# State-space tables one batch per piece of the first layer, held behind VectorE's last work

## The chip, the cores and the metric

The kernel runs on one core of a Trainium2 chip. The metric is the device time of one execution in microseconds; the time stated is the median of three runs. TensorE does the matmuls, VectorE and ScalarE the element-wise work and the reading of PSUM, GpSimd a part of the element-wise work, and SyncE issues most DMAs.

## What is computed

A network of four layers on x of [512 tokens, 2048 channels]: layer ab (gated linear attention beside forgetting attention), layer c (a state-space layer), an even layer (recurrence beside window attention) and an odd layer (two further attentions), with a norm ahead of each and one at the end. The change concerns the parameters of layer c, which depend on the weights alone:

```python
def s5_ssm(u, lam_re, lam_im, log_step, b_re, b_im, c_re, c_im, d):   # 128 groups of 16 channels, 64 states each
    step = jnp.exp(log_step)[:, None]
    mag = jnp.exp(lr * step)
    lb_re, lb_im = mag * jnp.cos(li * step), mag * jnp.sin(li * step)
    ...
    _, _, x_re, x_im = lax.associative_scan(_complex_combine, (a_re, a_im, bu_re, bu_im), axis=1)
    y = einsum('gcp,blgp->blgc', c_re, x_re) - einsum('gcp,blgp->blgc', c_im, x_im)
    return y + d * uf
```

The kernel writes the recurrence with powers of the complex factor. A table of angles holds, for the eight groups of a batch, the cosine and sine parts for 512 positions; it is the product of two small tables, so four products and two sums make it.

## The kernel before

**Projections.** Every projection is a sum of three matmuls on split operands (a high and a low part of weight and activation), `PARTS`, line 270. SyncE's queue loads a weight piece (`wraw`, three buffers), ScalarE writes its high part (`act`, line 137) and VectorE its low part (`tt`, line 140) into `whl` (four buffers), then TensorE runs 12 matmuls of 128x512 on it (`mm`, line 152), in `chunkF` (line 272) or `chunkT` (line 290). The sums stand in four PSUM banks `pj`. These loads and splits have a raised priority.

**Order.** A scheduler that simulates time sets the order of the instructions on each engine before the launch; on the chip each engine runs its own list in that order and waits by semaphores. Tiles come from a pool by name: a name has so many buffers (line 109), and a new tile takes the next buffer in the order in which the program asks for tiles, so its first writer waits for the last reader of the tile that had the buffer. `whl` has four, `hc` four, `vs` four, `fac`, `cst`, `acc`, `acc2` and `lm` one each. `after(...)` (line 159) adds a rule to the scheduler: what is issued in it comes behind the named instruction on the same engine.

**State-space parameters.** `params(o)` (line 1589) is called with o = 0 in layer ab, with 1 to 8 around the attention heads of its second half (`fox`, line 781), with 9 to 12 after the pieces of the gate, and with 13 to 20 after the eight pieces of `w_out` (line 444, the call is `beside(13 + o)`). There are 16 batches of eight groups.
- o = 0: the small tables of all batches go to memory (`s5tab`, `s5w`).
- o = 1 to 8: `s5_tables(2 * (o - 1))` (line 999) makes the tables of two batches: one load of 192 KB into `lm` (line 1004), and for each batch, on VectorE, twice `cst<-lm`, `acc<-lm` and the sum or difference `hc<-cst,acc`. The two `hc` are stored by ScalarE's queue as `s5ph` (lines 1020 and 1021).
- o = 3 to 18: `s5_batch_params(o - 3)` (line 1024) has two halves. The first loads two `vs` tiles and lets GpSimd make Z: `cst<-vs,vs` twice, `hc<-cst` twice, a store to `s5d`, and the same once more, then VectorE GG (`vs<-vs,smb`, `acc<-vs`, in the tile `acc2`), then GpSimd BB (`fac<-vs,smb`, `fac<-fac`). The profile names a tile by its tag without numbers, so GG reads as `acc` there. The second half, 32 small matmuls (`tr<-vs,fac`, `tr<-acc,fac`) and its stores, comes one call of `params` later.

`w_out` asks for a tile `acc` when it starts; GpSimd adds up squares in it (`acc<-acc,wt`) for the next norm, which reads it with eight matmuls `sc<-ones,acc` at the start of layer c. Layer c (line 1174) begins with `states(c_)` (line 1192): a chunk of 16 weight pieces by `chunkT`, whose sums ScalarE writes into two `vs` tiles (`vs<-pj,tk`), four `pj` banks at a time; the next chunk follows in the same banks. After it the recurrence of layer c reads `s5ph` and `s5d`.

## Time and profile before

| | us |
|---|---|
| median of three runs | 3410.19 (3409.04 to 3414.12) |
| the profiled execution's own time | 3407.61 |
| its span in the trace | 3405.8 |
| TensorE busy in it | 3349.1 (98%) |
| VectorE, ScalarE, GpSimd busy | 1907.8, 1337.7, 784.1 |

The profile is one execution on the chip. Times in its rows count from the start of the span. A busy TensorE is not TensorE at its peak: its granted clock is 1.00 of full speed (2.4 GHz) in most stretches and 0.96 on average between 480 and 800 us, where single runs of matmuls after a wait are at the lower level (1.2 GHz) for a part of their length. Idle time of an engine is put down to what ended it. The parameters of layer c are made from 490 us on, `w_out` of layer ab runs from about 791 to 975 us, and layer c starts with the norm at 983 us.

### The profile page before, as it was taken

To read this page: it belongs to the slowest core of one execution; us is meant where nothing else is said; L and a number is where in the kernel's file an instruction comes from. 1 tells how busy PE (TensorE), PEld (TensorE's weight loads), DVE (VectorE), ACT (ScalarE), POOL (GpSimd) and SP (SyncE) were. 2 spreads that over 40 slices of the span, in tenths; PEclk is the share of its full clock that TensorE was granted. 3 is DMA by queue.
4 is the path that set the end of the run, shared out by engine and by line. 5 is a ranking of instruction groups with operands and counts; after the bars stand their busy time and mean duration, and the time that the engine had idled before them with its cause. 6 is when DMAs were issued, how large, how long until landed. Compare 5 with 4: busy or idle time off the path is not lost.

```text
span 3405.8 us, 45778 instructions
## 1 busy us (share of the span) xinstructions
PE 3349.1 (98%) x16332; PEld 2722.4 (80%) x16332; DVE 1907.8 (56%) x3213; ACT 1337.7 (39%) x2497; POOL 784.1 (23%) x974
## 2 busy tenths in 40 slices
PE   9999999999999999999999999999999999999997
PEld 8888776777788888888888777888888788888885
DVE  5753457787556576834354655453544545647634
ACT  5443432233343333423343655232433444535532
POOL 0330364348602223200221100012110120212011
PEclk9999999999999999999999999999999999999999
DMA  5223335576634444343443223334333223332343
GB/s 156 72 69 91 87 109 159 169 218 207 206 107 132 135 144 141 116 121 118 145 127 90 66 75 90 94 120 145 105 92 81 73 65 81 80 88 75 106 120 106
DMA packets 389013, 390.01 MB, mean 115 GB/s; under 512 B 66968, under 2 KB 327448, under 8 KB 388784
## 3 DMA queue, kind: packets, MB, share of 16 engines
q1 hardware_dynamic: 362992, 354.64, 36.4%
q10 hardware_dynamic: 22464, 22.12, 1.9%
q0 software_dynamic: 3328, 10.32, 0.8%
q8 instruction: 128, 2.10, 0.3%
q14 instruction: 101, 0.83, 0.1%
HBM read 340.71 MB, written 46.25 MB: 114 GB/s over the span
## 4 chain that ended last, share of the span: by engine, by line
PE 73%; DVE 2%; POOL 1%; issue 1%; DMA 0%; DVEq 0%; ACT 0%; SPq 0%
PE pj L152 66%; PE sc L152 3%; PE po L152 3%; PE tr L156 1%; POOL wt L140 1%; DVE wk L140 0%; PE tr L152 0%; DVE hl L140 0%; DMA vs<-s5w 0%; DVE wk L1139 0%; DVE whl L140 0%; POOL cst L140 0%; DVE ha L143 0%; DVE sc L140 0%; DVE hc L143 0%
## 5 line engine op out<-in xcount | busy, mean ns | idle before, releaser
L152 PE MATMUL pj<-hl,whl 128*128 128x512 f32 x10224 | 2459.6, 398 | 14.8 <-DVE whl L140 7.3
L152 PEld LDWEIGHTS pj<-hl,whl 128*128 128x128 f32 x10224 | 1912.8, 189 | 456.3 <-DVE whl L140 10.2
L140 DVE TENSOR_TENSOR whl<-wraw,whl 128x512 fp32r<-128x512 f32 (+2 forms) x1064 | 805.3, 759 | 1082.7 <-ACT whl L137 1077.5
L137 ACT ACTIVATE whl<-wraw 128x512 fp32r<-128x512 f32 (+2 forms) x1064 | 661.5, 623 | 1353.9 <-PE pj L152 1096.6
L152 PE MATMUL pj<-whl,hl 128*128 128x512 f32 (+2 forms) x2112 | 466.1, 380 | 4.1 <-DVE whl L140 2.3
L152 PEld LDWEIGHTS pj<-whl,hl 128*128 128x128 f32 x2112 | 375.4, 191 | 81.4 <-DVE whl L140 3.1
L140 POOL TENSOR_TENSOR acc<-acc,wt 128x512 f32<-128x512 f32 x73 | 102.7, 1415 | 798.7 <-ACT wt L137 797.4
L137 ACT ACTIVATE wk<-sc,sm 128x256 f32<-128x256 f32 (+3 forms) x160 | 79.6, 502 | 90.3 <-DVE sm L148 86.8
L140 POOL TENSOR_TENSOR ha<-wk,ha 64x512 fp32r<-64x512 f32 x32 | 45.0, 1407 | 290.7 <-ACT ha L137 264.2
L140 POOL TENSOR_TENSOR wt<-wt,acc 64x508 f32<-64x508 f32 x32 | 63.9, 1995 | 181.4 <-DVE wt L140 125.7
L140 POOL TENSOR_TENSOR wt<-ha,wk 128x256 f32<-128x256 f32 x72 | 61.9, 888 | 127.4 <-PE sc L152 66.9
L152 PE MATMUL po<-pt,vs 128*128 128x128 f32 x560 | 80.0, 276 | 0.2
L152 PEld LDWEIGHTS po<-pt,vs 128*128 128x128 f32 x560 | 72.8, 192 | 3.2 <-ACT pt L137 0.8
L152 PE MATMUL sc<-ha,ha 128*128 128x128 f32 (+1 forms) x224 | 71.2, 390 | 3.5 <-DVE ha L140 2.7
L156 PE MATMUL tr<-ident,wk 128*128 128x128 f32 x416 | 71.4, 275 | 1.4 <-DVE pt L509 1.1
L137 ACT ACTIVATE pt<-tr 128x384 f32<-128x384 f32 (+3 forms) x96 | 46.7, 486 | 62.0 <-PE tr L156 60.1
L148 DVE TENSOR_SCALAR wk<-wk,sm 128x256 f32<-128x256 f32 (+3 forms) x160 | 65.4, 422 | 4.5
L140 POOL TENSOR_TENSOR fac<-wt,acc 128x512 fp32r<-128x512 f32 x8 | 10.8, 1353 | 244.3 <-ACT acc L137 130.3
L156 PEld LDWEIGHTS tr<-ident,wk 128*128 128x128 f32 x416 | 52.0, 141 | 18.8 <-issue 3.4
L137 ACT ACTIVATE ge<-ge 128x512 f32<-128x512 f32 x64 | 40.3, 630 | 66.7 <-DVE ge L140 55.7
L521 DVE TENSOR_REDUCE sm<-sc 128x1 f32<-128x128 f32 (+3 forms) x96 | 45.8, 487 | 34.1 <-PE sc L152 33.5
L140 POOL TENSOR_TENSOR cst<-vs,vs 128x256 f32<-128x256 f32 x64 | 53.5, 855 | 32.1 <-DMA vs<-s5w 18.8
(316 smaller groups left out, 2984.3 us busy)
## 6 DMA issues: line engine op xcount, KB each, us to landing
wraw<-in_l_w_in_dram SPq DMA_DIRECT2D x272, 256.0 KB, 2.8
wraw<-in_ab_w_in_dram SPq DMA_DIRECT2D x216, 256.0 KB, 2.8
wraw<-in_c_w_in_dram SPq DMA_DIRECT2D x128, 256.0 KB, 2.7
wraw<-in_l_w_out_dram SPq DMA_DIRECT2D x128, 256.0 KB, 2.9
wraw<-in_ab_w_out_dram SPq DMA_DIRECT2D x64, 256.0 KB, 3.4
wraw<-in_glu_w_dram SPq DMA_DIRECT2D x64, 256.0 KB, 2.9
wraw<-in_c_w_out_dram SPq DMA_DIRECT2D x64, 256.0 KB, 3.0
wraw<-in_l_w_in_dram SPq DMA_DIRECT2D x128, 128.0 KB, 2.3
```

Source lines behind the costliest of these rows:

```text
L137: return self.nc.scalar.activation(out, in_, func, **kw)
L140: return (eng or self.nc.vector).tensor_tensor(out, a, b, op=op)
L148: return e.tensor_scalar(out, a, s1, None, op0=op0)
L152: return self.nc.tensor.matmul(out, l, r, start=start, stop=stop)
L156: return self.nc.tensor.transpose(out, in_, self.ident[:k, :k])
L521: self.nc.vector.tensor_reduce(mx, pb[:, 0:w], axis=AX.X, op=ALU.max)
```

## The change

`s5_tables` makes one batch's table instead of two, and becomes a generator with two steps. It is called with o = 1 to 16 (so the last four tables fall among the first four pieces of `w_out`), with a load of 96 KB for each. The first step is held by `after` behind the last `tensor_tensor` that `tt` had issued on VectorE by then (`last_dve`), the second step, the two stores, behind the last instruction that `act` had issued on ScalarE (`last_act`), and it runs in the next call of `params`. In `params` the second steps that are pending now come first, then the table, then the batch.

```diff
--- before.py
+++ after.py
@@ -134,10 +134,14 @@
 
 
     def act(self, out, in_, func=AF.Copy, **kw):
-        return self.nc.scalar.activation(out, in_, func, **kw)
+        self.last_act = self.nc.scalar.activation(out, in_, func, **kw)
+        return self.last_act
 
     def tt(self, out, a, b, op, eng=None):
-        return (eng or self.nc.vector).tensor_tensor(out, a, b, op=op)
+        r = (eng or self.nc.vector).tensor_tensor(out, a, b, op=op)
+        if eng is None:
+            self.last_dve = r
+        return r
 
     def stt(self, out, a, s, b, op0, op1, **kw):
         return self.nc.vector.scalar_tensor_tensor(out, a, s, b, op0=op0, op1=op1, **kw)
@@ -996,30 +1000,31 @@
         self.own = self.cp.tile([P, 16], F32, name="own")
         nc.vector.tensor_reduce(self.own, self.ident.rearrange("p (a c) -> p c a", c=16), axis=AX.X, op=A.add)
 
-    def s5_tables(self, b0):
-
+    def s5_tables(self, b):
 
         nc, A = self.nc, ALU
-        tab = self.t("lm", [P, S])[:, 0:384].rearrange("p (b f) -> p b f", b=2)
-        self.dma.dma_start(tab, self.s5tab[b0:b0 + 2, :, 0:192].rearrange("b p f -> p b f"))
-        for b in range(2):
-            Tb = tab[:, b, 0:128].rearrange("p (i n q) -> p i n q", i=2, q=4)
-            Ta = tab[:, b, 128:192].rearrange("p (i n q) -> p i n q", i=2, q=4)
-            C, Sn = self.hd("hc"), self.hd("hc")
-            u = [self.t("cst", [P, S]), self.t("acc", [P, S])]
-            v4 = lambda ap: ap.rearrange("p (q a b) -> p q a b", q=4, a=8)
-            av = lambda i: Ta[:, i].rearrange("p n q -> p q n").unsqueeze(3).to_broadcast([P, 4, 8, 16])
-            bv = lambda i: Tb[:, i].rearrange("p n q -> p q n").unsqueeze(2).to_broadcast([P, 4, 8, 16])
+        tab = self.t("lm", [P, S])
+        self.dma.dma_start(tab[:, 0:192], self.s5tab[b][:, 0:192])
+        Tb = tab[:, 0:128].rearrange("p (i n q) -> p i n q", i=2, q=4)
+        Ta = tab[:, 128:192].rearrange("p (i n q) -> p i n q", i=2, q=4)
+        C, Sn = self.hd("hc"), self.hd("hc")
+        u = [self.t("cst", [P, S]), self.t("acc", [P, S])]
+        v4 = lambda ap: ap.rearrange("p (q a b) -> p q a b", q=4, a=8)
+        av = lambda i: Ta[:, i].rearrange("p n q -> p q n").unsqueeze(3).to_broadcast([P, 4, 8, 16])
+        bv = lambda i: Tb[:, i].rearrange("p n q -> p q n").unsqueeze(2).to_broadcast([P, 4, 8, 16])
+        with self.after([self.last_dve]):
             self.tt(v4(u[0]), av(0), bv(0), A.mult)
             self.tt(v4(u[1]), av(1), bv(1), A.mult)
             self.tt(C, u[0], u[1], A.subtract)
             self.tt(v4(u[0]), av(0), bv(1), A.mult)
             self.tt(v4(u[1]), av(1), bv(0), A.mult)
             self.tt(Sn, u[0], u[1], A.add)
-            d = self.dp.tile([P, 2, S], F32, name=self.name("s5ph"))
+        yield
+        d = self.dp.tile([P, 2, S], F32, name=self.name("s5ph"))
+        with self.after([self.last_act]):
             nc.scalar.dma_start(d[:, 0], C)
             nc.scalar.dma_start(d[:, 1], Sn)
-            self.s5ph.append(d)
+        self.s5ph.append(d)
 
     def s5_batch_params(self, b):
 
@@ -1591,15 +1596,16 @@
 
             if o == 0:
                 net.s5_params()
-            elif o <= 8:
-                net.s5_tables(2 * (o - 1))
             for b in pending:
                 with net.after([net.last]):
                     next(b, None)
             pending.clear()
+            if 1 <= o <= 16:
+                pending.append(net.s5_tables(o - 1))
+                next(pending[-1])
             if 3 <= o < 19:
                 pending.append(net.s5_batch_params(o - 3))
-                next(pending[0])
+                next(pending[-1])
         if "ab" in layers:
             h = net.layer_ab(raws, beside=params if "c" in layers else None)
             raws, acc, _ = net.w_out(h, I["ab_w_out"][0], beside=params if "c" in layers else None, **end("ab"))
@@ -1609,8 +1615,8 @@
             if "ab" not in layers:
                 net.s5_params()
                 for b in range(16):
-                    if b % 2 == 0:
-                        net.s5_tables(b)
+                    for _ in net.s5_tables(b):
+                        pass
                     for _ in net.s5_batch_params(b):
                         pass
             h = net.layer_c(raws, acc)
```

Instruction order on VectorE in the second half of layer ab, where the first tables stand (`whl<-wraw` are weight splits, `ha<-pj` evictions), before:

```order
L140 TENSOR_TENSOR cst_4050<-lm_4046 128x512
L140 TENSOR_TENSOR acc_4051<-lm_4046 128x512
L140 TENSOR_TENSOR whl_4620<-wraw_4618,whl_4620 128x512
L140 TENSOR_TENSOR ha_4572<-pj_4440,bc_230 128x512
L140 TENSOR_TENSOR hc_4048<-cst_4050,acc_4051 128x512
L140 TENSOR_TENSOR ha_4580<-pj_4441,bc_230 128x512
L140 TENSOR_TENSOR cst_4050<-lm_4046 128x512
L140 TENSOR_TENSOR acc_4051<-lm_4046 128x512
L140 TENSOR_TENSOR whl_4637<-wraw_4635,whl_4637 128x512
L140 TENSOR_TENSOR hc_4049<-cst_4050,acc_4051 128x512
L140 TENSOR_TENSOR whl_4654<-wraw_4652,whl_4654 128x512
L140 TENSOR_TENSOR cst_4063<-lm_4046 128x512
```

The same place after (the table here is the third one; four of its six instructions are shown):

```order
L141 TENSOR_TENSOR whl_4595<-wraw_4593,whl_4595 128x512
L141 TENSOR_TENSOR hc_4198<-cst_4200,acc_4201 128x512
L141 TENSOR_TENSOR whl_4612<-wraw_4610,whl_4612 128x512
L141 TENSOR_TENSOR cst_4200<-lm_4196 128x512
L141 TENSOR_TENSOR acc_4201<-lm_4196 128x512
L141 TENSOR_TENSOR hc_4199<-cst_4200,acc_4201 128x512
L141 TENSOR_TENSOR whl_4629<-wraw_4627,whl_4629 128x512
L141 TENSOR_TENSOR whl_4646<-wraw_4644,whl_4646 128x512
L141 TENSOR_TENSOR whl_4663<-wraw_4661,whl_4663 128x512
L141 TENSOR_TENSOR whl_4690<-wraw_4688,whl_4690 128x512
```

Before, table after table stands between the splits; after, the splits follow each other once the third table is through.

Instruction order on GpSimd at the end of `w_out` and the norm of layer c (`acc<-acc,wt` are w_out's squares, `tk` belongs to the norm, `cst<-vs,vs` and `hc<-cst` are Z), before:

```order
L140 TENSOR_TENSOR fac_8416<-fac_8416 128x128
L140 TENSOR_TENSOR fac_8416<-vs_8385,smb_8383 128x128 x2
L140 TENSOR_TENSOR fac_8416<-fac_8416 128x128
L140 TENSOR_TENSOR acc_7104<-acc_7104,wt_8559 128x512
L140 TENSOR_TENSOR acc_7104<-acc_7104,wt_8574 128x512
L140 TENSOR_TENSOR acc_7104<-acc_7104,wt_8739 128x512
L140 TENSOR_TENSOR acc_7104<-acc_7104,wt_8754 128x512
L348 TENSOR_TENSOR tk_8766<-tk_8764,mhalf 128x4
L1146 MEMSET wt_9232 128x4
```

The same place after:

```order
L141 TENSOR_TENSOR acc_7057<-acc_7057,wt_8755 128x512
L141 TENSOR_TENSOR acc_7057<-acc_7057,wt_8770 128x512
L352 TENSOR_TENSOR tk_8782<-tk_8780,mhalf 128x4
L1057 MEMSET hc_7262 128x512
L1057 MEMSET hc_7269 128x512
L141 TENSOR_TENSOR cst_7261<-vs_7253,vs_7254 128x256 x2
L141 TENSOR_TENSOR hc_7262<-cst_7261 64x4x64 x2
L1065 DMA s5d_7259<-hc_7262 128x512
L141 TENSOR_TENSOR cst_7261<-vs_7253,vs_7254 128x256 x2
L1151 MEMSET wt_9248 128x4
L1151 MEMSET wt_9249 128x4
L141 TENSOR_TENSOR hc_7269<-cst_7261 64x4x64 x2
```

Before, the parameters of the last batch (the last `fac`) are done ahead of w_out's last squares, and the norm follows; after, Z of batch 10 (`cst_7261`) stands behind the norm, and those of batches 11 to 15 behind that.

Instruction order on VectorE at the same norm (`tk<-sc` is the norm), before:

```order
L140 TENSOR_TENSOR whl_8920<-wraw_8918,whl_8920 128x512
L140 TENSOR_TENSOR whl_8937<-wraw_8935,whl_8937 128x512
L149 TENSOR_SCALAR tk_8764<-sc_8759 128x4
L140 TENSOR_TENSOR whl_8954<-wraw_8952,whl_8954 128x512
L140 TENSOR_TENSOR tk_8768<-tk_8766,tk_8768 128x4
L140 TENSOR_TENSOR wt_8772<-ident,tk_8768 128x512
L140 TENSOR_TENSOR wt_8775<-ident,tk_8768 128x512
L140 TENSOR_TENSOR whl_8971<-wraw_8969,whl_8971 128x512
L140 TENSOR_TENSOR whl_8988<-wraw_8986,whl_8988 128x512
```

After:

```order
L141 TENSOR_TENSOR whl_8953<-wraw_8951,whl_8953 128x512
L141 TENSOR_TENSOR acc_7244<-lm_7239 128x512
L153 TENSOR_SCALAR tk_8780<-sc_8775 128x4
L141 TENSOR_TENSOR hc_7241<-cst_7243,acc_7244 128x512
L141 TENSOR_TENSOR whl_8970<-wraw_8968,whl_8970 128x512
L141 TENSOR_TENSOR cst_7243<-lm_7239 128x512
L141 TENSOR_TENSOR acc_7244<-lm_7239 128x512
L141 TENSOR_TENSOR tk_8784<-tk_8782,tk_8784 128x4
L141 TENSOR_TENSOR wt_8788<-ident,tk_8784 128x512
L141 TENSOR_TENSOR hc_7242<-cst_7243,acc_7244 128x512
L141 TENSOR_TENSOR wt_8791<-ident,tk_8784 128x512
L141 TENSOR_TENSOR whl_8987<-wraw_8985,whl_8987 128x512
```

Before, only splits and the norm stand there; after, table 12 is made there from its second product on (its first, `cst_7243<-lm_7239`, stands 91 rows further up), and the rows that follow hold tables 13 to 15 between the splits.

Instruction order on TensorE at the end of the first chunk of layer c (`pj<-whl` with the next chunk's number from 9273 on), before:

```order
L152 MATMUL pj_8846<-whl_9107,hl_8825 128x512 x3
L152 MATMUL pj_8847<-whl_9107,hl_8825 128x512 x3
L152 MATMUL pj_8848<-whl_9107,hl_8825 128x512 x3
L152 MATMUL pj_8849<-whl_9107,hl_8825 128x512 x3
L152 MATMUL pj_9273<-whl_9279,hl_8780 128x512 x3
L152 MATMUL pj_9273<-whl_9296,hl_8783 128x512 x3
L152 MATMUL pj_9273<-whl_9313,hl_8786 128x512 x3
```

After (the next chunk's number is 9289):

```order
L156 MATMUL pj_8863<-whl_9123,hl_8841 128x512
L156 MATMUL pj_8864<-whl_9123,hl_8841 128x512 x3
L156 MATMUL pj_8865<-whl_9123,hl_8841 128x512 x3
L156 MATMUL tr_8375<-vs_8181,fac_8212 32x16 x8
L156 MATMUL tr_8375<-acc_8204,fac_8212 32x48 x8
L156 MATMUL tr_8595<-vs_8401,fac_8432 32x16 x4
L156 MATMUL pj_9289<-whl_9295,hl_8796 128x512 x3
L156 MATMUL pj_9289<-whl_9312,hl_8799 128x512 x3
L156 MATMUL pj_9289<-whl_9329,hl_8802 128x512 x3
```

Before, the next chunk follows the first one directly; after, matmuls of batches 14 and 15 stand between them.

## Rows read from the trace of the kernel before

**Rows 1.** Page, engines: busy us, share of the span, instructions.

```profile
PE 3349.1 (98%) x16332; PEld 2722.4 (80%) x16332; DVE 1907.8 (56%) x3213; ACT 1337.7 (39%) x2497; POOL 784.1 (23%) x974
```

**Rows 2.** Busy time by stretch: length; busy (instructions) of each engine; clock, DMA, GB/s.

```profile
480.00:720.00 240.00, 226.18 (x1090) 178.94 (x1090) 179.52 (x296) 67.13 (x143) 108.47 (x206) 0.96 0.59 170
720.00:800.00 80.00, 71.95 (x454) 55.54 (x452) 65.80 (x90) 28.67 (x57) 56.71 (x86) 0.96 0.65 199
```

**Rows 3.** TensorE's waits, 480 to 720 us: total, times, longest.

```profile
PE pj L152 <- DVE whl L140: 8.4, 5, 3.6
PE sc L152 <- DVE ha L140: 2.7, 1, 2.7
PE pj L152 <- DVE ha L140: 1.8, 1, 1.8
```

**Rows 4.** VectorE in order of time: start, length, instruction [idle before <- releaser].

```profile
492.70 1.07 DVE L140 TENSOR_TENSOR cst<-lm 128x512 f32<-128x512 f32 x1 [5.95 <-DMA lm<-s5tab]
...
495.34 0.69 DVE L140 TENSOR_TENSOR hc<-cst,acc 128x512 f32<-128x512 f32 x1
...
509.37 1.06 DVE L140 TENSOR_TENSOR cst<-lm 128x512 f32<-128x512 f32 x1 [3.66 <-DMA lm<-s5tab]
...
511.32 0.69 DVE L140 TENSOR_TENSOR whl<-wraw,whl 128x512 fp32r<-128x512 f32 x1
...
542.63 0.80 DVE L140 TENSOR_TENSOR vs<-vs,smb 128x256 f32<-128x256 f32 x2 [1.77 <-POOL wt L988]
...
862.42 2.05 DVE L140 TENSOR_TENSOR vs<-vs,smb 128x256 f32<-128x256 f32 x2
```

**Rows 5.** TensorE in order of time, 512 to 554 us.

```profile
512.07 13.16 PE L152 MATMUL pj<-hl,whl 128*128 128x512 f32 x48 [3.58 <-DVE whl L140]
...
544.09 9.58 PE L152 MATMUL pj<-whl,hl 128*128 128x512 f32 x30 [1.80 <-DVE ha L140]
```

**Rows 6.** TensorE in order of time, the wait for `fac` in the gate pieces.

```profile
785.70 0.31 PE L152 MATMUL tr<-vs,fac 128*32 128x16 f32 x8 [5.43 <-POOL fac L140]
785.82 0.53 PE L152 MATMUL tr<-acc,fac 128*32 128x48 f32 x16
786.28 10.81 PE L152 MATMUL pj<-hl,whl 128*128 128x512 f32 x35
```

**Rows 7.** TensorE in order of time, the norm and first chunk of layer c.

```profile
982.92 1.80 PE L152 MATMUL sc<-ones,acc 128*128 128x1 f32 x8
...
992.81 35.01 PE L152 MATMUL pj<-whl,hl 128*128 128x512 f32 x150
```

**Rows 8.** ScalarE in order of time, the last eviction of that chunk.

```profile
1022.63 0.87 ACT L137 ACTIVATE vs<-pj,tk 128x256 f32<-128x256 f32 x2
```

**Rows 9.** DMA issues: count, KB each, us to landing; and the table loads' issue, ns.

```profile
vs<-in_s_bc_dram SPq DMA_DIRECT2D x16, 448.0 KB, 3.9
...
lm<-s5tab SPq DMA_DIRECT2D x8, 192.0 KB, 3.4
...
L1004 SPq DMA_DIRECT2D lm<-s5tab x8: 366/372/385, 490.1 to 690.9; - x8
```

**Rows 10.** GpSimd in order of time, one batch in w_out.

```profile
846.29 1.88 POOL L140 TENSOR_TENSOR cst<-vs,vs 128x256 f32<-128x256 f32 x2 [1.05 <-DMA vs<-s5w]
...
850.74 1.44 POOL L140 TENSOR_TENSOR cst<-vs,vs 128x256 f32<-128x256 f32 x2
852.26 1.88 POOL L140 TENSOR_TENSOR hc<-cst 64x256 f32<-64x256 f32 x2
854.20 0.53 POOL L1052 MEMSET hc<- 128x512 f32 x1
...
861.37 1.39 POOL L140 TENSOR_TENSOR fac<-vs,smb 128x128 f32<-128x128 f32 x2
862.72 1.47 POOL L140 TENSOR_TENSOR acc<-acc,wt 128x512 f32<-128x512 f32 x1
...
865.95 0.52 POOL L140 TENSOR_TENSOR fac<-fac 128x128 f32<-128x128 f32 x1
```

## The prediction

> **What bounds the kernel now.** I read the page's engine line first, then the busy time by stretch around the work that the change touches, then TensorE's waits there, then the single rows of those waits. TensorE is busy for 3349.1 us [rows 1], 98% of the span, so only its idle time, its clock and the number of its instructions can move the end. In the 320 us in which the state-space parameters are prepared it is busy 226.18 of 240 us and 71.95 of 80 us [rows 2]: idle 13.8 + 8.05 = 21.9 us, more than a third of all its idle time (3405.8 - 3349.1 = 56.7 us). That is what a better placing of this work can take back. The waits say which work is late [rows 3]: in the first 240 us 8.4 us for `whl`, VectorE's split of a weight piece, 1.8 and 2.7 us for `ha`, also VectorE's. VectorE's own rows show why [rows 4]: a table is four products of about 1.08 us and two sums of 0.69 us, 5.7 us in all. One load feeds two tables; the next load can go only when both are done, and VectorE stands still for it (5.95 us, 3.66 us) with the splits queued behind. TensorE then runs dry at 508.5 us for 3.58 us [rows 5] and in five more places up to 544 us. In the last 80 us the largest wait is 5.43 us for `fac`, GpSimd's part of a batch [rows 6].
>
> **Part 1, tables one by one in the first layer: a gain.** The order before puts six tables and a half between the splits of 492 to 548 us; after the change three stand there, the next follow one per piece. The stores that now go one piece later fall out of ScalarE's row of weight copies. What that is worth:
> - The first wait stays and grows. Each table now waits for its own load. Loads of 192 KB land 3.4 us after issue [rows 9]; the tile `lm` has one buffer, so the load of table 1 goes after the last product of table 0, about 2 us before VectorE is through with the rest. The fourth split, which in the trace starts at 511.3 us [rows 4], comes about 1.6 us later. I book -1.6 us.
> - The five other waits of that stretch are 8.4 - 3.58 + 1.8 = 6.6 us [rows 3, 5]. The tables that caused them are gone from there, so I take 5 to 6.6 us as won, 3 to 5 net of the first line.
> - After each wait TensorE runs slowly for a while (granted clock 0.96 over the stretch [rows 2], a mean of its two levels 2.4 and 1.2 GHz): 48 matmuls in 13.16 us and 30 in 9.58 us [rows 5], against 150 in 35.01 us [rows 7], 0.233 each. Those two runs cost 13.16 - 11.2 = 2.0 and 9.58 - 7.0 = 2.6 us, and the short runs between them, by the same rate, some 2 more. I take 5 us as won. The stretch gives about 9.
> - Near 670 us, 2.7 us for `ha` and its slow clock [rows 3]: VectorE's order has two tables right before that `ha` before the change and none after it. I take 3.5 us.
> - The last 80 us (8.05 us) are bound by GpSimd: two batches' parts alternate with the gated pieces. Nothing that GpSimd does is removed. I take 1.5 us, with 6 either way.
> Together 14 us. The bounds are 7 and 32: all 21.9 us, and the slow clock of all its runs (2.0 + 2.6 + 2.0 here, 10.81 - 8.2 = 2.6 for the 35 matmuls behind the wait for `fac` [rows 6], about 1 at 670).
>
> The Trainium skill speaks against the split loads: "DMA: Bandwidth & Descriptors", section "Anatomy of one DMA", fits a DMA as a fixed 2.0 us plus its bytes over 436 GB/s. By it half the bytes land an estimated 0.2 us sooner, so sixteen loads would wait almost twice as long as eight. The trace has 3.4 us for 192 KB and nothing for 96 KB here; my -1.6 us already takes the load as no shorter.
>
> **Part 2, the tables of the last four batches slip behind w_out: a loss.** This is the larger term. The table's second product goes into a tile `acc`, of which there is one buffer. Before, all sixteen tables are asked for by o = 8, before w_out asks for the same buffer as its sum of squares. After, w_out asks first, at its start, and tables 12 to 15 (o = 13 to 16) come behind it. That buffer is read by the `sc<-ones,acc` matmuls at the start of layer c, which end at t0 = 982.92 + 1.80 = 984.7 us [rows 7]. So these four tables cannot run inside w_out at all; the order of VectorE shows them behind the norm. And table 12 has its first product in `cst` by then, the one buffer through which GpSimd's part Z of each batch also goes. So Z of batches 10 to 15 also moves behind t0, where it alternates with the tables: table 12, Z 10, table 13, Z 11, table 14, Z 12, table 15, Z 13, Z 14, Z 15.
>
> Who waits for that: `states(0)`, the first chunk of layer c, is evicted by ScalarE into two `vs` tiles. `vs` has four buffers, a batch holds two; the two that `states(0)` gets are those of batch 14. Its eviction must wait until Z 14 has read them, and the first matmul of the next chunk needs the PSUM bank that this eviction frees. Before, that bank was free in time: the last eviction of the chunk starts at 1022.63 us [rows 8] while TensorE runs on, that is t0 + 37.9. After, from t0:
> - Table 12's rest: three products and two sums, 4.6 us, and two splits and the norm's small work between them: +6.3.
> - Z 10: 846.29 to 852.26 + 1.88, 7.85 us [rows 10]: +14.2.
> - Then three periods (Z 11, Z 12, Z 13). Table and Z share `cst`: 5.7 + 7.85 = 13.55 us is the least. On GpSimd's side: the next batch's `vs` comes free at the last read, 850.74 + 1.44, 2.0 us before the end of Z; its reload lands after 3.9 us [rows 9], so 2 us after it; then `fac`, 861.37 to 866.47 with 1.47 us of w_out's squares in it, so 3.6 us; two memsets of 0.53; Z: 14.7 us. On VectorE's side two to four splits of 0.69 us stand among a table's products: 15 to 16. I take 15.6, because those splits have to be made in any case: +61.0.
> - Z 14 up to its last read, with the `fac` of batch 15 interleaved in GpSimd's order: 5.9 + two of its products, one sum and a memset, about 9: +70.
> - Two evictions, 0.87 us [rows 8]: the next chunk starts at t0 + 71.
> TensorE has all its work of `states(0)` done at t0 + 37.9, so it idles about 33 us, partly already before the chunk's last piece, whose split stands behind table 14 in VectorE's order. From that comes off what four batches' small matmuls cost when they stood inside w_out: 785.70 to 786.28 us for 24 of a batch's 32 [rows 6], about 0.75 a batch, 3 us, which now fill the wait. That leaves 30 us. The slow clock behind a wait costs 2.0 to 2.6 us in the three runs above; I add 2.5: **32.5 us lost**. From below: with the least period, 14.2 + 40.7 + 5.9 + 0.9 = 61.7, so 61.7 - 37.9 - 3 = 21, with the clock 23. From above: if table and `fac` also go one after the other, the period is 5.7 + 3.6 + 1.1 + 7.85 = 18.3, and 14.2 + 54.9 + 11 + 0.9 = 81, 40 us, with the clock 42.
>
> The trace shows that VectorE and GpSimd hinder each other: the pair `vs<-vs,smb` took 0.80 us at 542.63 and 2.05 us at 862.42, beside GpSimd's `fac` [rows 4, 10]. The Trainium skill, "SBUF — State Buffer", section "Who interferes with whom", says more: a VectorE instruction with two SBUF inputs and a GpSimd instruction that reads SBUF exclude each other for the whole instruction. By that rule the time goes to the upper bound, which is the second rival.
>
> **Part 3, nothing.** Storing one piece later, recording the last instruction in `act` and `tt`, and eight more DMA issues on SP's queue (0.37 us each [rows 9], with a weight load queued behind) move no work of TensorE: 8 x 0.37 = 3 us spread over 300, hidden by weight pieces that are loaded three ahead. `after([self.last_dve])` orders the table behind VectorE's last recorded work. Queued behind it on VectorE are the next splits; the held table costs them no more than the tables did before.
>
> **The sum.** 3407.6 us was the profiled execution's own time, 2.6 below the median of 3410.2. 3407.6 - 14 + 32.5 = 3426; on the median's footing **3429 us**.
>
> **The rivals.**
> - *The wait cancels the gain.* The chain runs at its least period (23 us) and the early stretch gives 16 to 30. What speaks for it: VectorE's order has few splits left in the stretch once TensorE has stopped. Against: 14.7 us on GpSimd's side alone. Net -7 to +7: 3403 to 3417.
> - *Faster.* All waits of 480 to 800 us vanish, with their slow clock: 32 us; the chain costs 23. Net -9, 3401 us. It decides from the point where the last 80 us become smooth, since GpSimd, no longer given two tables' worth of loads at once, would start each batch earlier. Against it: 5.43 us of that stretch are GpSimd's own length, which the change leaves as it is.
> - *Table and `fac` exclude each other.* Period 18.3: lost 42, won 14, net +28, up to +36 where the early gain is the low 7: 3438 to 3446. For it: 2.05 against 0.80 us above. Against: in 861 to 866 us GpSimd's own instructions grew by far less.
> - *The change doesn't do what it says.* "Held behind VectorE's last work" only orders VectorE. Where the tables come after that is up to `acc`. If w_out's sum of squares did not hold it, tables 12 to 15 would run inside w_out, where TensorE waits for nothing; then there is no late loss and the time is 3410 - 14 = 3396. The instruction order speaks against it, since it has those rows behind the norm; I count it with "faster".
>
> **Chances.** A measurement can tell about 0.2% of this kernel, 6.8 us, from no change. Forecast, net +10 to +28 (3420 to 3438): 0.60. Table and `fac` exclude each other, or longer still: 0.18. Cancelling, -7 to +7: 0.12. Faster, including the fourth rival: 0.06. The rest, +7 to +10: 0.04. Slower is 0.60 + 0.18 + 0.04 = 0.82, the same 0.12, faster 0.06. The range reaches from 3409, which leaves out "faster" and half of "cancelling", to 3446, which leaves out some 0.06 of the long chains: 0.18 left out.
>
> **What would show it.** Right: a wait of 25 to 40 us of TensorE some 30 us into layer c, released by an eviction or by GpSimd's `cst`; no table on VectorE inside w_out but for the first product of table 12, four behind the norm; Z of six batches behind it, one each 15 to 16 us; the five waits between 525 and 545 us gone, the one near 508 us still there. Wrong: tables 12 to 15 before t0; Z 14 done by t0 + 50; a new wait in w_out, where Z of batches 10 to 15 is missing; or waits at 750 to 790 us that have grown by more than 6 us.

## The result

The changed kernel takes 3443.4 us (3442.8 to 3443.8) against 3410.9 us (3409.0 to 3414.1): 32.5 us more, ratio 1.0095 with a 95% interval of 1.0083 to 1.0108. The forecast was 3429, the range 3409 to 3446. The profiled execution took 3443.6 us, 36.0 more than that of before, and the accounts below are on that footing.

First the page's engine line of the changed kernel, the answer to [rows 1], then the busy time by stretch, the answer to [rows 2] (length; busy time and instructions of TensorE, its weight loads, VectorE, ScalarE, GpSimd; granted clock, DMA share, GB/s):

```profile
PE 3357.8 (98%) x16332; PEld 2722.8 (79%) x16332; DVE 1904.2 (55%) x3213; ACT 1339.8 (39%) x2497; POOL 798.1 (23%) x974
```

```profile
480.00:720.00 240.00, 235.90 (x1205) 188.24 (x1203) 144.41 (x261) 73.16 (x154) 106.45 (x210) 1.00 0.56 162
720.00:800.00 80.00, 69.72 (x412) 52.49 (x412) 70.81 (x102) 25.80 (x51) 57.41 (x72) 0.91 0.59 177
800.00:900.00 100.00, 96.62 (x494) 76.51 (x493) 53.02 (x72) 28.09 (x49) 38.06 (x44) 0.98 0.58 183
1000.00:1100.00 100.00, 70.42 (x397) 55.81 (x396) 65.62 (x93) 23.28 (x46) 63.85 (x91) 0.81 0.51 156
```

Between 480 and 720 us TensorE's idle time has fallen from 13.8 to 4.1 us and its granted clock is 1.00 instead of 0.96. From 720 to 800 us it is worse than before (69.72 busy instead of 71.95, clock 0.91 instead of 0.96), from 800 to 900 it idles 3.4 us, and from 1000 to 1100 us it is idle for 29.6 us, at a clock of 0.81 of full speed, a mean of its two levels. So there is a gain, a give-back, and a large new wait. TensorE's waits (total, times, longest), the answer to [rows 3]: the first row is from 480 to 720 us, the next two from 720 to 970 us, the last from 970 to 1060 us:

```profile
PE pj L156 <- DVE whl L141: 2.9, 3, 1.5
...
PE pj L156 <- DVE whl L141: 6.9, 5, 4.7
PE tr L156 <- DVE acc L141: 4.4, 3, 2.8
...
PE tr L156 <- POOL fac L141: 27.9, 6, 12.9
```

How far the program has come is read from instructions that both kernels have: the first mask matmul of the attention heads, the third eviction of the gate pieces, w_out's first evictions. Before (TensorE, then VectorE twice):

```profile
588.11 0.22 PE L152 MATMUL sc<-maskb,identb 128*128 128x128 bf16 x1
...
727.83 0.69 DVE L140 TENSOR_TENSOR ge<-pj,bc 128x512 f32<-128x512 f32 x1
...
815.02 1.27 DVE L140 TENSOR_TENSOR rawa<-pj,wk 128x512 f32<-128x512 f32 x2
```

After:

```profile
574.81 0.22 PE L156 MATMUL sc<-maskb,identb 128*128 128x128 bf16 x1
...
710.78 0.69 DVE L141 TENSOR_TENSOR ge<-pj,bc 128x512 f32<-128x512 f32 x1
...
807.41 1.28 DVE L141 TENSOR_TENSOR rawa<-pj,wk 128x512 f32<-128x512 f32 x2
```

The changed kernel is 13.3 us ahead at the first, 17.0 at the second, and only 7.6 at the third. At the norm of layer c it is 8.7 us ahead (974.22 against 982.92 in [rows 7]), with four batches' small matmuls moved behind that point. TensorE's rows, the answer to [rows 5 to 7], show both ends:

```profile
510.62 8.64 PE L156 MATMUL pj<-hl,whl 128*128 128x512 f32 x36 [1.47 <-DVE whl L141]
...
532.30 41.82 PE L156 MATMUL pj<-whl,hl 128*128 128x512 f32 x178 [0.89 <-DVE whl L141]
...
794.62 7.79 PE L156 MATMUL pj<-hl,whl 128*128 128x512 f32 x22 [4.72 <-DVE whl L141]
...
974.22 1.80 PE L156 MATMUL sc<-ones,acc 128*128 128x1 f32 x8
...
1053.79 7.51 PE L156 MATMUL pj<-whl,hl 128*128 128x512 f32 x22 [2.51 <-ACT vs L137]
```

The first wait of [rows 5], 3.58 us, is 1.47 us, and 178 matmuls run at full speed (41.82 / 178 = 0.235) where 30 ran slowly. With t0 = 974.22 + 1.80 = 976.02, the second chunk of layer c starts at 1053.79 = t0 + 77.8; before, the first chunk's last eviction started at t0 + 37.9 [rows 8] while TensorE ran on. Measured from there it is 39.9 us later, of which 8.7 were ahead, so 31.2; its first 22 matmuls take 7.51 us where 22 x 0.233 = 5.1 are needed, 2.4 more. TensorE does not stand there in one wait: the batches' small matmuls come ahead of the second chunk, and most of the idle time (27.9 us in six waits, the longest 12.9) is put down to their `fac`. The last wait is released by ScalarE's eviction, and that by GpSimd's `cst`, as ScalarE's row says:

```profile
1052.90 1.20 ACT L137 ACTIVATE vs<-pj,tk 128x256 f32<-128x256 f32 x3 [6.34 <-POOL cst L141]
```

### The profile page after: what moved, and what is told of

Read it like the earlier page. It is cut to its first block, busy times and chain, and to the rows that moved or that the text cites. A ratio compares the mean times of both kernels' runs of the same rounds, so it can differ in the third digit from the quotient of the medians.

```text
span 3441.8 us, 45796 instructions
## 1 busy us (share of the span) xinstructions
PE 3357.8 (98%) x16332; PEld 2722.8 (79%) x16332; DVE 1904.2 (55%) x3213; ACT 1339.8 (39%) x2497; POOL 798.1 (23%) x974
## 4 chain that ended last, share of the span: by engine, by line
PE 86%; POOL 5%; DVE 5%; DMA 2%; issue 1%; ACT 0%; ACTq 0%; DVEq 0%; SPq 0%; POOLq 0%
PE pj L156 76%; PE sc L156 4%; PE po L156 3%; PE tr L160 1%; POOL cst L141 1%; POOL fac L141 1%; POOL hc L141 1%; POOL wt L141 1%; DVE acc L141 1%; DMA vs<-in_s_bc_dram 1%; DVE whl L141 1%; POOL vs L141 1%; PE tr L156 0%; DVE hl L141 0%; DMA s5d<-vs 0%
## 5 line engine op out<-in xcount | busy, mean ns | idle before, releaser
L156 PEld LDWEIGHTS pj<-hl,whl 128*128 128x128 f32 x10224 | 1911.4, 189 | 463.6 <-DVE whl L141 12.6
## 6 DMA issues: line engine op xcount, KB each, us to landing
wraw<-in_l_w_in_dram SPq DMA_DIRECT2D x128, 128.0 KB
```

What stands on the lines that cost most here:

```text
L156: return self.nc.tensor.matmul(out, l, r, start=start, stop=stop)
```

## What happens behind the norm and in the gate pieces

GpSimd in order of time in the changed kernel, the answer to [rows 10]: first a Z in the gate pieces, then the first rows of Z 10 to 13 behind the norm, the `fac` between two of them, and the second pair of Z 14 while VectorE does nothing:

```profile
776.93 6.65 POOL L141 TENSOR_TENSOR cst<-vs,vs 128x256 f32<-128x256 f32 x2 [8.61 <-DVE hc L141]
...
981.90 4.00 POOL L141 TENSOR_TENSOR cst<-vs,vs 128x256 f32<-128x256 f32 x2 [2.10 <-DVE hc L141]
...
1000.01 1.72 POOL L141 TENSOR_TENSOR cst<-vs,vs 128x256 f32<-128x256 f32 x2 [0.30 <-DVE hc L141]
...
1012.87 1.77 POOL L141 TENSOR_TENSOR fac<-vs,smb 128x128 f32<-128x128 f32 x2 [2.98 <-DMA vs<-in_s_bc_dram]
...
1018.52 2.59 POOL L141 TENSOR_TENSOR cst<-vs,vs 128x256 f32<-128x256 f32 x2
...
1036.57 1.64 POOL L141 TENSOR_TENSOR cst<-vs,vs 128x256 f32<-128x256 f32 x2
...
1051.46 1.41 POOL L141 TENSOR_TENSOR cst<-vs,vs 128x256 f32<-128x256 f32 x2
```

Z starts at 981.90, 1000.01, 1018.52 and 1036.57: periods of 18.1, 18.5 and 18.1 us instead of 15.6. Z 11 waits 0.30 us for a table; Z 12 and Z 13 wait for nothing but GpSimd's own instructions before them. So it is mostly GpSimd's own steps that are longer: `fac` from 1012.87 to 1018.1, 5.2 us with a memset of 0.5 in it, 4.7 instead of 3.6; Z from 1000.01 to 1009.2, 9.2 instead of 7.85; the reload lands 2.98 us after GpSimd has become idle, where 2.0 was forecast. Over the three periods (54.7 us, where the prediction's steps on GpSimd's side make 43.4) Z up to its last read takes 5.3 us more, `fac` with the memsets 3.6, and the reload 2.3 (3.6, 5.6 and 4.8 us from its issue to `fac`, where 3.9 was taken). A pair `cst<-vs,vs` takes 4.00 us at 981.90 and 1.41 at 1051.46. VectorE's rows beside the long one:

```profile
978.46 1.08 DVE L141 TENSOR_TENSOR cst<-lm 128x512 f32<-128x512 f32 x1
...
982.32 0.70 DVE L141 TENSOR_TENSOR whl<-wraw,whl 128x512 fp32r<-128x512 f32 x1
982.92 1.08 DVE L141 TENSOR_TENSOR acc<-lm 128x512 f32<-128x512 f32 x1
983.92 0.68 DVE L141 TENSOR_TENSOR whl<-wraw,whl 128x512 fp32r<-128x512 f32 x1
```

During those 4.00 us, behind the last 0.5 us of an earlier instruction, VectorE runs a split, a product of table 13 and another split, 0.70 + 1.08 + 0.68 = 2.46 us, at their usual lengths; 1.41 + 2.46 = 3.87. The pair took about its own length plus that of the three instructions beside it, as if the two engines had gone one after the other. That fits the rule of the Trainium skill, "SBUF — State Buffer", section "Who interferes with whom": a VectorE instruction with two SBUF inputs contends with a GpSimd instruction that reads SBUF, for a port pair that only one of them holds at a time. The trace agrees here, with 4.00 against 3.87.

In the gate pieces the row at 776.93 shows the same, longer: GpSimd had waited 8.61 us for a table's `hc` (the table had the one `cst`), and then its pair took 6.65 us among VectorE's instructions. In return VectorE's next table waits 5.39 us for Z, with the weight splits queued behind; TensorE's wait of 4.72 us at 794.62 follows:

```profile
790.17 1.06 DVE L141 TENSOR_TENSOR cst<-lm 128x512 f32<-128x512 f32 x1 [5.39 <-POOL hc L141]
```

## The experiments

**Free `acc`.** Tables 12 to 15 leave `acc` to w_out.

```diff
-u = [self.t("cst", [P, S]), self.t("acc", [P, S])]
+u = [self.t("cst", [P, S]), self.t("ge" if b >= 12 else "acc", [P, S])]
```

> The changed kernel, but tables 12 to 15 take their second product in a tile `ge`, which w_out does not use, instead of `acc`. Theory (w_out's `acc` holds these four tables): they run inside w_out, Z of all batches is done before the norm, TensorE's wait of about 40 us in front of the second chunk of layer c is gone, and what is left is the gain before w_out, some 5 us: 3400 to 3411. Rival (GpSimd has too little time for the batches inside w_out whatever the tables do): Z of several batches still runs behind the norm, a wait of 15 us or more stays there, 3425 to 3443.

Measured: 3415.6 us, ratio to the kernel before 1.0021 (1.0012 to 1.0031), 28 us faster than the changed kernel. The wait in front of the second chunk is gone, so w_out's `acc` is what held the four tables. But the time is 5 us above the expected range: the kernel is 10.6 us ahead of the one before at w_out's first eviction and 7.2 us behind at the norm. In between lie three waits for `whl` of 2.7 to 3.6 us, behind each of which 46 matmuls take 12.4 to 13.8 us instead of 10.7. TensorE's waits from 790 us on (the longest stands ahead of that eviction):

```profile
PE pj L156 <- DVE whl L141: 13.3, 5, 4.1
```

**Free `acc` and `cst`.** Is it VectorE's wait for `cst`, or the table itself, that costs 18 us in w_out?

```diff
-u = [self.t("cst", [P, S]), self.t("acc", [P, S])]
+u = [self.t("ge" if b >= 12 else "cst", [P, S]), self.t("ge" if b >= 12 else "acc", [P, S])]
```

> The changed kernel with both products of tables 12 to 15 in tiles `ge`, so that these tables share neither `acc` with w_out's squares nor `cst` with Z. With `acc` freed alone 18 us were still lost inside w_out, in four waits for `whl`. If VectorE stood there for `cst` with the splits queued behind it, those waits go and the time is 3396 to 3406. If the table itself (5.7 us in front of the splits, held there) is the cause, it stays at 3411 to 3417.

Measured: 3416.2 us, 1.0025 (1.0015 to 1.0035), the same as the run before. So the shared `cst` is not what costs in w_out. VectorE, GpSimd and ScalarE in this run, ahead of a wait of 4.30 us for `whl` at 852 us:

```profile
837.96 2.73 DVE L141 TENSOR_TENSOR ge<-lm 128x512 f32<-128x512 f32 x2
...
845.43 5.17 DVE L141 TENSOR_TENSOR ge<-lm 128x512 f32<-128x512 f32 x2
...
851.07 0.88 DVE L141 TENSOR_TENSOR whl<-wraw,whl 128x512 fp32r<-128x512 f32 x1
...
845.78 1.41 POOL L141 TENSOR_TENSOR cst<-vs,vs 128x256 f32<-128x256 f32 x2
847.14 1.27 POOL L141 TENSOR_TENSOR acc<-acc,wt 128x512 f32<-128x512 f32 x1
848.37 1.30 POOL L141 TENSOR_TENSOR fac<-fac 128x128 f32<-128x128 f32 x1
...
841.28 4.91 ACTq L1098 DMA_DIRECT2D s5d<-vs  x2
846.29 0.63 ACT L137 ACTIVATE whl<-wraw 128x512 fp32r<-128x512 f32 x1 [5.22 <-DMA s5d<-vs]
```

Two products of a table take 5.17 us (2 x 1.08 alone) beside three GpSimd rows of 1.41 + 1.27 + 1.30 us, so 3.0 us more beside 4.0 us, and the next split comes at 851.07. A table of 5.7 us is spread over 15 us, 837.96 to 853. ScalarE shows a second thing. Its row of 4.91 us spans two stores whose issues take 0.33 us each; the second one stands from 841.6 to 845.87 us until a semaphore lets it go, and the weight copy behind it waits 5.22 us. Which of the two delays makes TensorE's wait is not separated.

**Free `cst` alone.** Tables 12 to 15 still wait for `acc`, but no longer hold `cst`.

```diff
-u = [self.t("cst", [P, S]), self.t("acc", [P, S])]
+u = [self.t("ge" if b >= 12 else "cst", [P, S]), self.t("acc", [P, S])]
```

> The changed kernel, but tables 12 to 15 take their first product in a tile `ge` instead of `cst`; the second stays in `acc`, so they still wait for w_out. If the alternation of table and Z in the one `cst` sets the period of about 18 us behind the norm, Z no longer waits for a table, the period falls to GpSimd's own 14 to 15 us, and the time by 3 x 3.5 = 10 us or more: 3425 to 3433. If GpSimd's own steps (reload, `fac`, memsets, Z) fill the 18 us, nothing moves: 3440 to 3446.

Measured: 3442.3 us, 1.0101 (1.0086 to 1.0116), no different from the changed kernel. Its colsum and the start of the second chunk:

```profile
972.76 1.80 PE L156 MATMUL sc<-ones,acc 128*128 128x1 f32 x8
...
1052.21 7.88 PE L156 MATMUL pj<-whl,hl 128*128 128x512 f32 x27 [4.80 <-ACT vs L137]
...
1049.71 1.21 ACT L137 ACTIVATE vs<-pj,tk 128x256 f32<-128x256 f32 x3 [6.21 <-DVE acc L141]
```

1052.21 - 974.56 = 77.65 us, as in the changed kernel, but the end of the chain is another one. With `cst` free the first pair of Z 10 runs ahead of the norm (829.23), and the last read of Z 14 ends at 1044.21 = t0 + 69.7 instead of t0 + 76.9; the eviction then waits for VectorE's GG of batch 15, whose store stands ahead of it on ScalarE. So the equal time alone says nothing about `cst`. The periods do: from Z 11 to Z 13 two of them take 38.1 us (36.6 in the changed kernel), from Z 12 to Z 14 27.2 (27.1). The alternation of table and Z in one `cst` does not set the period; it does cost at the start, where Z 10 stands behind table 12.

**Short tables.** The disputed term by itself: tables 12 to 15 keep their waits but are made for a quarter of their positions, about 2 us of VectorE instead of 5.7; layer c reads tables 4 to 7 in their place.

```diff
+w = 4 if b < 12 else 1          # 128 * w of 512 positions, in products, sums and stores
+C, Sn, u = C[:, 0:128 * w], Sn[:, 0:128 * w], [x[:, 0:128 * w] for x in u]
...
-self.s5ph.append(d)
+self.s5ph.append(d if b < 12 else self.s5ph[b - 8])
```

> The changed kernel, with tables 12 to 15 computed and stored for a quarter of their positions (128 of 512 columns; layer c reads tables 4 to 7 in their place). Waits and order stay, VectorE's 5.7 us per table become about 2. If the tables lengthen the 18 us period behind the norm, by standing in it or by hindering GpSimd's `fac` and Z, the period falls to 14.5 to 16 us and the second chunk of layer c starts at t0 + 62 to 70: 3427 to 3435. If GpSimd's steps and the reload alone make the period, only table 12's own 4 us go: 3438 to 3441.

Measured: 3432.5 us, 1.0071 (1.0056 to 1.0086), 11 us faster than the changed kernel. The first rows of Z 10 to 13, and TensorE's colsum and next chunk:

```profile
977.09 2.11 POOL L141 TENSOR_TENSOR cst<-vs,vs 128x256 f32<-128x256 f32 x2
...
992.73 1.79 POOL L141 TENSOR_TENSOR cst<-vs,vs 128x256 f32<-128x256 f32 x2
...
1004.96 1.61 POOL L141 TENSOR_TENSOR cst<-vs,vs 128x256 f32<-128x256 f32 x2
...
1022.75 1.96 POOL L141 TENSOR_TENSOR cst<-vs,vs 128x256 f32<-128x256 f32 x2 [6.49 <-DVE hc L141]
...
972.63 1.80 PE L156 MATMUL sc<-ones,acc 128*128 128x1 f32 x8
...
1043.38 7.76 PE L156 MATMUL pj<-whl,hl 128*128 128x512 f32 x22 [2.51 <-ACT vs L137]
```

The periods are 15.6, 12.2 and 17.8 us, 15.2 on average instead of 18.2 (the last has 6.49 us in which GpSimd waits for a table's `hc`, another wait than in the changed kernel), and the chunk starts at 1043.38 - 974.43 = t0 + 69.0 instead of 77.8. Together with the run that frees `cst`: it is the work of the tables on VectorE, not their place in `cst`, that lengthens the period. That it does so by lengthening GpSimd's instructions is read from single rows; a later reload, or VectorE's GG kept waiting behind a table, is not separated from it. This run also shortens the table that stands first, so it does not separate the two to the last microsecond.

**Without tables 8 to 15.** They are neither made nor stored; layer c reads tables 0 to 7 a second time.

```diff
-if 1 <= o <= 16:
+if 1 <= o <= 8:
...
+net.s5ph += net.s5ph[0:8]      # ahead of layer c
```

> The changed kernel without tables 8 to 15: they are neither computed nor stored, and layer c reads tables 0 to 7 a second time in their place. If what is lost again between 727 and 815 us and in w_out comes from the tables there (each alternates with Z in the one `cst`, and VectorE stands before it with splits queued behind), the 17 us that are won by 727 us are kept to the norm: 3391 to 3398. Rival (GpSimd is late with the batches in the gate pieces with or without tables): half of them are lost again, 3402 or more.

Measured: 3393.2 us, 0.9958 (0.9942 to 0.9975). Its colsum and the busy time in a part of w_out:

```profile
964.53 1.80 PE L156 MATMUL sc<-ones,acc 128*128 128x1 f32 x8
...
800.00:900.00 100.00, 100.00 (x549) 80.20 (x548) 56.45 (x80) 29.59 (x57) 73.19 (x103) 1.00 0.69 228
```

It is 18.4 us ahead at the norm and w_out runs without a gap. So what is lost between 727 and 815 us comes from tables 8 to 15; whether they cost where they stand, or by making GpSimd's batches late, this run does not say. With tables 0 to 7 placed as in the change, some 15 us (3408.2 - 3393.2) is, as an estimate, the most that a placing of tables 8 to 15 can bring.

**Two tables per piece.** The other parts of the change stay (loads of 96 KB, hold, later store).

```diff
-if 1 <= o <= 16:
-    pending.append(net.s5_tables(o - 1))
-    next(pending[-1])
+if 1 <= o <= 8:
+    for b in (2 * o - 2, 2 * o - 1):
+        pending.append(net.s5_tables(b))
+        next(pending[-1])
```

> The changed kernel with two tables per piece for o = 1 to 8, as before the change; the loads of 96 KB, the hold and the later store stay. If one table per piece is what won 13 us by 588 us, they are lost again here and the time is near the kernel before: 3405 to 3415, with waits for `whl` and `ha` between 505 and 545 us. If the smaller loads, the hold or the later store won them, 3393 to 3402.

Measured: 3415.4 us, 1.0020 (1.0011 to 1.0030), just above the expected range. The lead at the first mask matmul falls from 13.3 to 4.6 us, and at the third gate eviction it is 1.1. TensorE's waits from 480 to 720 us are back:

```profile
PE pj L156 <- DVE whl L141: 4.8, 4, 2.1
PE sc L156 <- DVE ha L141: 4.3, 1, 4.3
```

So most of the early gain is the division, one table per piece; 4.6 of the 13.3 us come from the rest. The rest also costs: the run is still 0.8 us ahead at w_out's first eviction and 6.2 behind at the norm, with no table on VectorE after 796 us. Z has slipped into w_out: GpSimd is busy for 128.0 of the 175 us from 815 to 990 us, 90.9 in the kernel before.

**No hold.**

```diff
-with self.after([self.last_dve]):
+with ExitStack():
```

> The changed kernel without the hold of the tables behind VectorE's last work. If making one table per piece is what won 17 us by 697 us and the hold adds nothing, 3437 to 3450. If the hold won it, the tables come earlier on VectorE between the weight splits, waits for `whl` between 500 and 700 us come back, and the time is 3450 to 3465. The late wait stays in both.

Measured: 3447.4 us, 1.0116 (1.0101 to 1.0131), against the changed kernel's 1.0095 (1.0083 to 1.0108). The lead at the first mask matmul is 11.5 us instead of 13.3, at the last one 13.9 instead of 17.0, at w_out's first eviction 0.4 instead of 7.6, at the norm 5.7 instead of 8.7. So the hold wins 2 to 7 us on the way; at the end the medians differ by 4.1 us, and the intervals overlap.

**Other divisions.** All tables asked for before w_out: two per gate piece, or one each for o = 1 to 3 and two or three per piece later.

```diff
-if 1 <= o <= 16:
+if 1 <= o <= 12:                                                        # first run
+    for b in (o - 1,) if o <= 8 else (2 * o - 10, 2 * o - 9):
+for b in {1: (0,), 2: (1,), 3: (2,), 4: (3, 4), ..., 8: (11, 12), 9: (13,), 10: (14,), 11: (15,)}.get(o, ()):   # second
+for b in {1: (0,), 2: (1,), 3: (2,), 4: (3, 4), 5: (5, 6, 7), ..., 8: (14, 15)}.get(o, ()):   # third
```

> The changed kernel, with tables 8 to 15 made two per gate piece (o = 9 to 12), so that all are asked for before w_out asks for `acc`. Theory: the late wait is gone as with another tile; the gate pieces, where VectorE and GpSimd share `cst`, become tighter, 0 to 10 us more lost there than in the changed kernel: 3403 to 3420. Rival (the late wait has another cause): 3435 or more.

> The changed kernel with another division: one table per piece for o = 1 to 3, where the pieces follow closely, two for o = 4 to 8, one for o = 9 to 11. All tables are asked for before w_out's `acc`, so the late wait is gone, and the 13 us won by 588 us stay; three tables stay in the gate pieces. 3397 to 3406. If the attention pieces cannot take two tables each, waits for `whl` and `ha` come back there: 3407 to 3413.

> As the run before, but one table each for o = 1 to 3 and all others for o = 4 to 8 (2, 3, 3, 3, 2), none in the gate pieces, as in the kernel before. If the tables in the gate pieces are what costs there, this is the fastest: 3394 to 3402. If three tables per attention piece are too many, the loss moves there: 3403 to 3413.

Measured: 3412.4 (1.0013, 1.0003 to 1.0022), 3414.3 (1.0020, 1.0011 to 1.0029) and 3415.6 us (1.0022, 1.0013 to 1.0032). None has the late wait, which fits `acc` as its cause. All three keep the 13 us at the first mask matmul and lose them later: the first in the gate pieces and w_out (18.8 us of waits for `fac`), the second with 4.15 us for `ha` at 658 us and `fac` after it, the third with 3.37 and 2.96 us among the attention heads and `fac` to the end of w_out. The expected gains of the second and third were wrong.

The third run shows a way of losing that the changed kernel does not. No table is on VectorE after 804 us, yet the lead of 12.0 us at w_out's first eviction becomes 6.9 us behind at the norm (10.7 to -5.0 and 8.5 to -8.0 in the other two). TensorE's waits from 815 to 990 us in it:

```profile
PE tr L156 <- POOL fac L141: 10.1, 8, 4.5
```

GpSimd is busy for 135.8 of these 175 us, 90.9 in the kernel before: Z, which shares `cst` with the tables, is late: 12 of its 32 pairs `cst<-vs,vs` have started by 815 us, 21 in the kernel before. So a table need not stand in w_out to cost there.

**A version meant to beat both.** Tables 0 to 7 as in the change, none in the first three gate pieces, tables 8 to 15 with o = 12 to 19 in `ge`; then the same with each late table cut in two halves four splits apart.

```diff
-if 1 <= o <= 16:
-    pending.append(net.s5_tables(o - 1))
+if 1 <= o <= 8 or 12 <= o <= 19:
+    pending.append(net.s5_tables(o - 1 if o <= 8 else o - 4))
...
+u = [self.t("ge" if b >= 8 else "cst", [P, S]), self.t("ge" if b >= 8 else "acc", [P, S])]
```

> A version meant to beat both: tables 0 to 7 one per piece in the attention pieces as in the changed kernel, none in the gate pieces but the last, tables 8 to 15 one per piece with o = 12 to 19, that is in w_out, with both products in tiles `ge`. If Z and the tables hinder each other mainly through `cst`, and w_out has room on VectorE, the 18 us that the run without tables 8 to 15 kept are mostly kept here: 3392 to 3402. If a table in front of a piece's splits costs 3 us of waits each in w_out, 3410 to 3420.

> The version with tables 8 to 15 in w_out, but each such table is cut in two: its first three instructions come at the end of a piece, the other three are held behind the split of the seventh of the next piece's eight weight loads, four splits later. If the 14 us that the uncut version lost in w_out come from 5.7 us of table in front of the splits at once, half of them return: 3393 to 3400. If they come from the added work itself (VectorE and GpSimd hindering each other, more stores on ScalarE's queue), 3401 to 3406.

Measured: 3404.0 us, 0.9991 (0.9982 to 1.0000), and 3409.7 us, 0.9996 (0.9987 to 1.0005). Both lie outside the ranges expected of them. The first is 39 us faster than the changed kernel and 3 to 4 us faster than the kernel before, about 0.1%, with an interval that reaches 1: hardly clear of no change. It keeps 19.3 us at the third gate eviction and 5.2 at the norm; 14 are lost in w_out, 8.2 of them in seven waits for `whl` from 796 to 978 us. Its waits from 480 to 1000 us (that for `fac` stands in the gate pieces):

```profile
PE pj L156 <- DVE whl L141: 12.4, 13, 2.6
PE tr L156 <- POOL fac L141: 4.3, 1, 4.3
```

Cutting the tables brings no time back: in w_out itself 11.8 us are lost instead of 13.8, and the lead at its first eviction is 12.6 instead of 19.0. So it is for the most part the added work that costs, not 5.7 us in one piece. Whether by VectorE and GpSimd hindering each other or by more stores on ScalarE's queue is not separated.

## Why the prediction was right, and where it was off

The direction, the mechanism of the late loss and the range were right. The size was not: +32.5 us is above the forecast's own +10 to +28 and lies where a rival stood that had 0.18.

- **What bounds the kernel** was read rightly: idle time and slow clock in 480 to 720 us were there to be taken, 17.0 us of them by 727 us.
- **Part 1, the attention pieces.** Forecast 9 + 3.5 us, measured 17.0. The mis-sized term is the first wait: it was to grow by 1.6 us and fell from 3.58 to 1.47. The premise, loads no shorter than 3.4 us, was wrong: table 1's load is issued at 497.50 and its first product starts at 499.86, table 2's at 505.37 and 507.86, so 2.4 to 2.5 us, about 1 us less than the median for 192 KB. The Trainium skill's fit in "DMA: Bandwidth & Descriptors", section "Anatomy of one DMA", gives an estimated 0.2 us for it; it is given there for DMAs that GpSimd issues, these loads are on SyncE's queue, and the measurement decides.
- **Part 1, the last 80 us.** Forecast +1.5 with 6 either way, measured 17.0 - 7.6 = 9.4 us lost. This step failed. Its reason, "nothing that GpSimd does is removed", left out what is added: tables 8 to 11 now stand in the gate pieces. The run without tables 8 to 15 keeps 17.0 us and shows that tables are the cause; it does not separate 8 to 11 from those behind them (with 12 to 15 shortened 12.0 us are kept). That the sum of part 1 is off by no more than 14 against 7.6 is luck in part: 4.5 us too little before and 10.9 too much behind partly cancel.
- **w_out** was taken as a stretch in which TensorE waits for nothing. Of the 100 us from 800 on 3.4 are idle in the changed kernel, and a table there costs 1.8 us (14 us for eight in the version of 3404 us) to 4.5 us (17.8 us for four with `acc` freed), if all is put down to the tables that stand there; the third of the other divisions lost 18.9 us there without one. From 815 us to the norm the kernel gains 1.1 us, where four batches' matmuls moved away had been priced at 3.
- **Part 2, the late loss.** The mechanism held at each step: w_out's `acc` holds tables 12 to 15 (the run that frees it), table 12's rest ends and Z 10 starts at t0 + 5.9 (forecast 6.3), the eviction waits for Z 14, the second chunk waits for the eviction. The mis-sized term is the period, 15.6 forecast and 18.1 to 18.5 measured (GpSimd's steps, put at 14.7, add up to 14.5 as named, and on average each of them was longer); the chunk starts at t0 + 77.8 instead of 71. The slow clock behind it is 2.4 us, 2.5 forecast.
- **The rivals.** The period is that of "table and `fac` exclude each other", 18.3 us, and so is its loss, 42 forecast and 39.9 + 2.4 - 1.1 = 41.2 measured; its time, 3438 to 3446, holds the result. Its sum is met by luck in part: it has table, `fac` and Z one after the other at their usual lengths, while in the trace they overlap, are longer where they do, and the reload takes its share. The reason given against it, that GpSimd's instructions had grown by far less in 861 to 866 us, was drawn from one place and did not hold at others. "Cancelling" and "faster" are out. In the fourth rival the condition was right and the time wrong: with `acc` free the late loss is gone, but the time is 3416 instead of 3396, since the tables cost in w_out.
- **The sum** on the profile's footing: forecast -14 - 3 + 33 + 2.5 = 18.5 us; measured -8.7 + 39.9 + 2.4 = 33.6 of 36.0. Of the other 2.4 us 1.2 are lost by the `tr<-ident,vs` at 1123.43 us, which is 34.8 us late (1088.64 before); the rest comes further on in layer c and stays open.

## What to carry to other kernels

A new call in an old rotation of buffers changes who waits for whom: before moving a step, list the tiles it asks for and who asks next, since with one buffer the order of asking is the order of running. Work that is off the critical path still has a price where it and another engine lengthen each other: look up what runs beside it at the new place, and how long the same instruction takes there and alone. An equal time does not show that nothing has moved: read where the chain ends in each run. And taking apart a burst wins only as long as the pieces go to places with room on both engines.

## What the runs showed of the hardware that was not expected

VectorE's products and GpSimd's instructions lengthen each other by most of the length of what runs beside them: 4.00 instead of 1.41 us for a GpSimd pair beside 2.46 us of VectorE, up to 6.65 in the gate pieces, and 5.17 instead of 2.16 for two VectorE products beside 3.98 us of GpSimd. Half the bytes were there about 1 us sooner: 2.4 to 2.5 us from a load's issue to the first product for 96 KB, a median of 3.4 us to landing for 192 KB. A store on ScalarE's queue that stood for a semaphore held the weight copy behind it for 5.22 us, though issuing it takes 0.33.
